# A two-layer hybrid decoder on one core: other places for the steps of prepared units, tables and scores, and more units turned by TensorE

## The chip, the core and the metric

The kernel runs on one core of a Trainium2 chip. The metric is the device time of one execution in microseconds; lower is better. TensorE is called PE, VectorE DVE, ScalarE ACT, GpSimd POOL and SyncE SP, as in the profile.

## The reference

Two layers over x of 256 positions and 2048 channels, all in float32:

```python
h = rms_norm(x, mix_norm[l]);  proj = h @ w_in[l]            # -> q, k, v, u and v of the SGU, gate logits
q, k = rope(rms_norm(q)), rope(rms_norm(k))                  # 16 query heads, 4 key heads, width 64
branch_a = sliding_window_attention(q, k, v, sinks) @ w_attn_branch[l]   # window 128
branch_b = (u * (tril(w_s) @ layer_norm(v) + b_s)) @ w_sgu_branch[l]     # u, v through gelu; chunks of 128
x = x + (gate_a * branch_a + gate_b * branch_b) @ w_out[l]   # gates: sigmoid of the logits
h2 = rms_norm(x, ffn_norm[l])
x = x + (silu(h2 @ w_gate[l]) * (h2 @ w_up[l])) @ w_down[l]  # inner width 5632
```

## The kernel before

**Products.** All products of activations and weights run as float32 split in two: a weight piece becomes whi (rounded, by ACT, line 203) and wlo (the rest, by DVE, line 204), an activation piece uh and ul, and PE adds three products, whi with uh, wlo with uh, whi with ul (lines 289 to 291). The activations stand still in PE, turned so that channels lie on partitions; weights of 512 columns are streamed. The weights come as one long list of pieces of 256 rows by 512 columns, called entries here, 1010 in all; PE takes one after the other. For an entry that serves both halves of the 256 positions PE runs 12 matmuls. `Stream.next` loads pieces 7 entries ahead by SP's queue and splits them 4 entries ahead (W_SPLIT = 4); there are four whi and four wlo tiles (pool `wsp`).

**Units.** The activations of 512 channels, split and turned, are a unit. `transposed` makes one, in either of two ways. With `on_pe` PE turns it with eight transposes into PSUM (pt, line 398), and ACT and DVE split it from there. Otherwise DVE transposes blocks of 32 by 32 into a box (`turn`, line 357), 16 DMAs of POOL's queue gather the blocks into tt (line 362), and ACT and DVE split tt. There is one box tile for all turns.

**Units with four sums.** Pairs of products (gate and up; neighbouring columns of w_out and of w_down) use a scheme that saves one of eight products over the first 512 channels. For it the first unit of such a group (WINO = 0) is made in more steps: ACT copies tt into flat in two steps (`scaled`), ACT and DVE split flat into uh and ul, DVE forms four sums of 128 by 256 (line 438), and ACT and DVE split the sums into sh and sl (`finished`, line 429 and 430). DVE also forms four sums of weight pieces for each pair (line 191). Within a pair the accumulator of one half is copied out twice by ACT, into a tile called snap (line 315), before PE adds on to it.

**Order.** PE's order is written out by hand. Small work beside the products is put in place with `after(n, fn)`: fn is called n steps later, a step being 12 matmuls, and its instructions are issued behind the latest split of that time (`tick`). ACT, DVE, POOL and SP then run the order that a scheduler made of this; each engine's queue runs in order.

**Stages of a layer.** The input projection (kv, two q, v, u and gate chunks), beside which attention and the spatial gating run in steps: rotation of q and k, turning, then from Q_FIRST = 14 steps after a q chunk the scores (psc, line 683), five steps later the transposes of the weights (ppt), three steps later the weighted values (po, line 722). Then the products of the attention branch, the second gates and the gating branch; the output projection in two pairs (`residual`), whose chunks also feed the four units of the next norm (`Norm.unit`); eleven pairs of gate and up (`hidden`) in rounds of 4, 4 and 3, each followed by two pairs of w_down over the units of that round. Only the last unit of the round of three is turned by PE, and of the norms the last unit, in the second layer's first norm the last two. `prepare` loads a layer's small rows by POOL's queue, and six steps later `tables` multiplies the rotation tables by the q and k norm weights; for the second layer that begins 20 steps after the first layer's output projection.

## Time and profile before

| | |
|---|---|
| median of 3 runs | 2565.43 us (2562.68 to 2568.48) |
| the profiled execution | 2568.65 us, its span 2566.9 us |
| mean granted PE clock in it | 0.986 |
| PE busy | 2496.1 us (97%), 11102 instructions |
| DVE busy | 1912.0 us (74%) |
| ACT busy | 1341.9 us (52%) |
| weights and inputs read | 475.27 MB, 186 GB/s over the span |

In the lists of waits a row tells who waited for whom, then the total, the times and the longest in microseconds. In a table of stretches a row has the stretch, its length, then for PE, PE's weight loads, DVE, ACT and POOL the busy time and the number of instructions, the granted clock, the DMA share and GB/s. In a list in order of time a row has start, duration, engine, line, operation, and in brackets the idle time before it with what ended it. Lines are those of the kernel before.

### The profile page before, as it was taken

The page shows a single profiled execution, that of the slowest core. Times are in us where ns is not written, and L with a number is a line of the kernel's source. Part 1 is how long each engine was busy: PE and PEld are TensorE (multiplying, and loading weights), DVE is VectorE, ACT ScalarE, POOL GpSimd, SP SyncE. Part 2 cuts the span into 40 slices and gives each one's busy share as a digit, 9 for nine tenths or more (in the row PEclk, how much of TensorE's full clock was granted, in tenths as well). Part 3 has the DMA queues.
Part 4 walks back from the last instruction along what each step waited for, and adds up shares of the span by engine and source line. Part 5 has one row for each costly group of instructions (what it writes and reads, how often), then busy time and mean ns, then how long its engine had stood idle before and what let it go on. Part 6 is the DMA issues. An engine that isn't in the chain of part 4 may idle for free. (4 is left out here: it accounts for less than half of the span.)

```text
span 2566.9 us, 31129 instructions
## 1 busy us (share of the span) xinstructions
PE 2496.1 (97%) x11102; PEld 2055.7 (80%) x11102; DVE 1912.0 (74%) x2291; ACT 1341.9 (52%) x1658; POOL 420.4 (16%) x815
## 2 busy tenths in 40 slices
PE   9899999999899999999998999999999999999999
PEld 7788888878787878787877888888787888788877
DVE  6686556887777778687976865567887777877787
ACT  5455444565555555455644554445655555555554
POOL 2401222121120112001124012221211201120110
PEclk9999999999999999999999999999999999999999
DMA  8655666565575757566666556665666666575754
GB/s 282 190 157 171 199 206 211 187 215 189 188 223 170 224 166 227 171 211 192 214 193 191 157 172 198 207 209 177 219 193 192 222 192 209 185 232 181 222 166 154
DMA packets 274123, 504.62 MB, mean 197 GB/s; under 512 B 27248, under 2 KB 29904, under 8 KB 273968
## 3 DMA queue, kind: packets, MB, share of 16 engines
q1 hardware_dynamic: 248720, 476.90, 58.8%
q0 software_dynamic: 24928, 25.47, 3.4%
q8 instruction: 87, 1.43, 0.2%
q14 instruction: 68, 0.56, 0.1%
q10 hardware_dynamic: 320, 0.27, 0.0%
HBM read 475.27 MB, written 2.10 MB: 186 GB/s over the span
## 5 line engine op out<-in xcount | busy, mean ns | idle before, releaser
L204 DVE TENSOR_TENSOR wlo<-raw,whi 128x1024 fp32r<-128x1024 f32 (+1 forms) x1012 | 1229.1, 1220 | 572.9 <-ACT whi L203 562.4
L203 ACT ACTIVATE whi<-raw 128x1024 fp32r<-128x1024 f32 (+1 forms) x1012 | 1065.8, 1058 | 1054.7 <-PE acc L291 861.8
L289 PE MATMUL acc<-whi,uh 128*128 128x512 f32 x3204 | 1261.6, 394 | 8.0 <-ACT uh L380 3.3
L291 PE MATMUL acc<-whi,ul 128*128 128x512 f32 x3204 | 1254.9, 392 | 7.4 <-DVE ul L381 4.8
L290 PE MATMUL acc<-wlo,uh 128*128 128x512 f32 x3204 | 1254.5, 392 | 1.2 <-DVE wlo L204 1.2
L291 PEld LDWEIGHTS acc<-whi,ul 128*128 128x128 f32 x3204 | 605.8, 189 | 137.4 <-DVE ul L381 6.5
L289 PEld LDWEIGHTS acc<-whi,uh 128*128 128x128 f32 x3204 | 606.9, 189 | 135.9 <-ACT uh L380 4.2
L290 PEld LDWEIGHTS acc<-wlo,uh 128*128 128x128 f32 x3204 | 606.8, 189 | 129.4 <-DVE wlo L204 4.1
L362 POOL DMA_DIRECT2D tt<-box x736 | 362.1, 499 | 1753.5 <-DVE box L357 561.3
L191 DVE TENSOR_TENSOR raw<-raw,raw 128x1024 f32<-128x1024 f32 x152 | 185.4, 1220 | 0.8
L289 PE MATMUL acc<-whi,sh 128*128 128x512 f32 x304 | 122.3, 402 | 35.1 <-ACT snap L315 35.1
L291 PE MATMUL acc<-whi,sl 128*128 128x512 f32 x304 | 121.9, 401 | 0.0
L290 PE MATMUL acc<-wlo,sh 128*128 128x512 f32 x304 | 121.4, 399 | 0.0
L315 ACT ACTIVATE snap<-acc 128x512 f32<-128x512 f32 x114 | 68.0, 596 | 59.5 <-PE acc L291 59.5
L289 PEld LDWEIGHTS acc<-whi,sh 128*128 128x128 f32 x304 | 58.4, 192 | 50.4 <-ACT snap L315 38.5
L291 PEld LDWEIGHTS acc<-whi,sl 128*128 128x128 f32 x304 | 58.8, 193 | 12.6
L290 PEld LDWEIGHTS acc<-wlo,sh 128*128 128x128 f32 x304 | 58.7, 193 | 11.8
L812 DVE SCALAR_TENSOR_TENSOR xs<-acc,xs 128x512 f32<-128x512 f32 (+1 forms) x66 | 42.5, 668 | 9.9 <-PE acc L291 9.9
L883 DVE TENSOR_TENSOR snap<-acc,snap 128x512 f32<-128x512 f32 x66 | 45.3, 686 | 4.5 <-PE acc L291 4.2
L812 DVE SCALAR_TENSOR_TENSOR xs<-snap,xs 128x512 f32<-128x512 f32 (+1 forms) x50 | 33.0, 663 | 2.1 <-ACT snap L315 2.0
L687 DVE TENSOR_TENSOR pr<-psc,mask 128x256 f32<-128x256 f32 (+1 forms) x32 | 17.3, 552 | 23.1 <-PE psc L683 23.1
L381 DVE TENSOR_TENSOR ul<-tt,uh 128x512 fp32r<-128x512 f32 x52 | 33.5, 683 | 0.0
(134 smaller groups left out, 891.2 us busy)
## 6 DMA issues: line engine op xcount, KB each, us to landing
raw<-in_w_in_dram SPq DMA_DIRECT2D x239, 512.0 KB, 4.0
raw<-in_w_up_dram SPq DMA_DIRECT2D x176, 512.0 KB, 4.9
raw<-in_w_gate_dram SPq DMA_DIRECT2D x176, 512.0 KB, 4.3
raw<-in_w_down_dram SPq DMA_DIRECT2D x176, 512.0 KB, 4.5
raw<-in_w_out_dram SPq DMA_DIRECT2D x64, 512.0 KB, 4.7
tt<-box POOLq DMA_DIRECT2D x736, 32.0 KB, 4.3
raw<-in_w_attn_branch_dram SPq DMA_DIRECT2D x32, 512.0 KB, 4.0
raw<-in_w_sgu_branch_dram SPq DMA_DIRECT2D x32, 512.0 KB, 4.4
```

The source lines that it names most:

```text
L191: self.last = nc.vector.tensor_tensor(out=self.raws[d], in0=self.raws[x], in1=self.raws[y], op=ALU.add if op == "+" else ALU.subtract)
L203: nc.scalar.activation(hi[:, i, :], raw[:, i, :], AF.Copy)
L204: self.last = nc.vector.tensor_tensor(out=lo[:, i, :], in0=raw[:, i, :], in1=hi[:, i, :].bitcast(F32), op=ALU.subtract)
L289: nc.tensor.matmul(ps, a, hi[:, kk, :], start=first and kk == 0, stop=False, skip_group_check=True)
L290: nc.tensor.matmul(ps, a, lo[:, kk, :], start=False, stop=False, skip_group_check=True)
L291: nc.tensor.matmul(ps, b, hi[:, kk, :], start=False, stop=kk == 1, skip_group_check=True)
L315: nc.scalar.activation(p.snaps[tag], a[1], AF.Copy)
L362: nc.gpsimd.dma_start(dst[j * B:(j + 1) * B, i], box[i * B:(i + 1) * B, j])
L381: nc.vector.tensor_tensor(out=l, in0=s_, in1=h.bitcast(F32), op=ALU.subtract)
L687: nc.vector.tensor_tensor(out=pr[:, :, j, :nk], in0=pscore[:, :, :nk], in1=mk.unsqueeze(1).to_broadcast([P, 2, nk]), op=ALU.add)
L812: nc.vector.scalar_tensor_tensor(out=xs[:, t, sl], in0=part[:, i * w:(i + 1) * w], scalar=scale, in1=xs[:, t, sl], op0=ALU.mult, op1=ALU.add)
L883: nc.vector.tensor_tensor(out=x[1], in0=x[0], in1=x[1], op=ALU.add)
```

## The change

Four things, with no change to what is computed:

- A unit with four sums takes its six steps (two copies, the split, two halves of the sums, the split of the sums) at distances of its own for each of the three kinds: WINO_NORM, WINO_MIX and WINO_HID. Before, they were 6, 7, 8 (split and all sums) and 9 for all.
- `tables` runs in two steps, five and six steps after `prepare`, and the second layer's `prepare` comes 28 instead of 20 steps after the output projection.
- Q_FIRST is 16 instead of 14, so scores, weighted values and the turn of the attention output come two steps later.
- The last unit of every round of hidden units is turned by PE (four more), three steps after its product, and so is unit 1 of the second layer's first norm; the last unit of that norm is turned two instead of three steps after its chunk.

```diff
+WINO_NORM = 7, 8, 10, 11, 12, 13
+WINO_MIX = 6, 7, 9, 10, 11, 13
+WINO_HID = 7, 8, 17, 18, 19, 20
...
-Q_FIRST = 14
+Q_FIRST = 16
...
-        def sums():
-            split_(uh, ul, flat["a"])
-            flat["s"] = ss = slot([P, 4, 2, P], name="sums")
+        def sums(n):
+            if n == 0:
+                flat["s"] = slot([P, 4, 2, P], name="sums")
+            ss = flat["s"]
...
-                                  (2, a11, a21, ALU.subtract), (3, a12, ss[:, 1], ALU.subtract)):
+                                  (2, a11, a21, ALU.subtract), (3, a12, ss[:, 1], ALU.subtract))[2 * n:2 * n + 2]:
...
-        after(6, lambda: scaled(0))
-        after(7, lambda: scaled(2))
-        after(8, sums)
-        after(9, finished)
+        for n, fn in zip(wino, (lambda: scaled(0), lambda: scaled(2), lambda: split_(uh, ul, flat["a"]),
+                                lambda: sums(0), lambda: sums(1), finished)):
+            after(n, fn)
...
-        after(6, pl.tables)
+        after(5, lambda: pl.tables(0))
+        after(6, lambda: pl.tables(1))
...
-                after(3 if j == NCH - 1 else 2, lambda: nxt.unit(j, j == NCH - 1 or j == NCH - 2 and not nxt.wino))
+                after(3 if j == NCH - 1 and nxt.wino else 2, lambda: nxt.unit(j, j == NCH - 1 or j > 0 and not nxt.wino))
...
-            after(2 + (j == NCH - 1), lambda j=j: transposed(mT, j, ga[j], on_pe=j == NCH - 1, wino=j == WINO))
+            after(2 + (j == NCH - 1), lambda j=j: transposed(mT, j, ga[j], on_pe=j == NCH - 1, wino=WINO_MIX if j == WINO else None))
...
-            after(20, lambda: prepare(l + 1))
+            after(28, lambda: prepare(l + 1))
...
-                pe = c == len(hT) - 1 == 2
-                after(3 if pe else 2, lambda: transposed(hT, c, hid, on_pe=pe, wino=c == WINO))
+                pe = c == len(hT) - 1
+                after(3 if pe else 2, lambda: transposed(hT, c, hid, on_pe=pe, wino=WINO_HID if c == WINO else None))
```

More of the change, by code (lines that the diff above doesn't have):

```diff
@@ L365, in turn, with transposed @@
         after(1, lambda: (blocks(1), gather()))
-    def transposed(units, c, src, cols=None, on_pe=False, wino=False):
+    def transposed(units, c, src, cols=None, on_pe=False, wino=None):
         uh = slot([P, 4, S], F32R, "uh")
@@ L466, in unit @@
             transposed(self.units, c, xs[:, :, c * CW:(c + 1) * CW], cols=self.cols[:, 4 * c:4 * c + 4],
-                       on_pe=on_pe, wino=self.wino and c == WINO)
+                       on_pe=on_pe, wino=WINO_NORM if self.wino and c == WINO else None)
         def finish(self):
@@ L557, in fetch, with tables, signs @@
                     self.lnb = dst
-        def tables(self):
+        def tables(self, i):
+            l, gn = self.l, self.gn
+            if i == 0:
+                self.signs()
+            ca = lay.tile([P, NT, 2, H2], F32, tag=f"ca{i}", name=f"ca{l}_{i}")
+            sa = lay.tile([P, NT, 2, H2], F32, tag=f"sa{i}", name=f"sa{l}_{i}")
+            for t in range(NT):
+                for hf in range(2):
+                    g_same = gn[:, i, hf * H2:(hf + 1) * H2]
+                    g_other = gn[:, i, (1 - hf) * H2:(2 - hf) * H2]
+                    nc.vector.tensor_tensor(out=ca[:, t, hf, :], in0=cs[:, t, :], in1=g_same, op=ALU.mult)
+                    nc.vector.scalar_tensor_tensor(out=sa[:, t, hf, :], in0=sn[:, t, :],
+                                                   scalar=-1.0 if hf == 0 else 1.0, in1=g_other,
+                                                   op0=ALU.mult, op1=ALU.mult)
+            self.rope.append((ca, sa))
+        def signs(self):
             l, gn = self.l, self.gn
@@ L564, in tables @@
             self.rope = []
-            for i in range(2):
-                ca = lay.tile([P, NT, 2, H2], F32, tag=f"ca{i}", name=f"ca{l}_{i}")
-                sa = lay.tile([P, NT, 2, H2], F32, tag=f"sa{i}", name=f"sa{l}_{i}")
-                for t in range(NT):
-                    for hf in range(2):
-                        g_same = gn[:, i, hf * H2:(hf + 1) * H2]
-                        g_other = gn[:, i, (1 - hf) * H2:(2 - hf) * H2]
-                        nc.vector.tensor_tensor(out=ca[:, t, hf, :], in0=cs[:, t, :], in1=g_same, op=ALU.mult)
-                        nc.vector.scalar_tensor_tensor(out=sa[:, t, hf, :], in0=sn[:, t, :],
-                                                       scalar=-1.0 if hf == 0 else 1.0, in1=g_other,
-                                                       op0=ALU.mult, op1=ALU.mult)
-                self.rope.append((ca, sa))
         def spatial(self):
```

## The prediction

> **What bounds the kernel now.** I read the page first, then the chain that ended last, the waits of PE alone, a table of stretches around each long wait, and the instructions in order of time at three of them.

> ```profile
> span 2566.9 us, 31129 instructions
> PE 2496.1 (97%) x11102; PEld 2055.7 (80%) x11102; DVE 1912.0 (74%) x2291; ACT 1341.9 (52%) x1658; POOL 420.4 (16%) x815
> ```

> PE is busy in 97% of the span, no other engine in more than 80%. So only two things can move the time: work that PE does, and gaps of PE. The waits of PE (us in total, times, longest us) name the gaps:

> ```profile
> PE acc L289 <- ACT snap L315: 35.1, 8, 7.7
> PE psc L683 <- ACT qT L667: 14.1, 2, 7.1
> PE acc L291 <- DVE ul L381: 4.8, 4, 1.4
> ```

> A gap costs more than its idle time. Stretches around every gap (us; busy us and count by engine; PEclk is the granted clock), with an undisturbed one last:

> ```profile
> 94.00:110.00 16.00, 8.89 (x34) 6.95 (x33) 8.55 (x13) 3.35 (x5) 6.22 (x8) 0.79 0.37 116
> 550.00:560.00 10.00, 6.78 (x23) 5.19 (x22) 7.58 (x14) 4.68 (x8) 4.36 (x9) 0.83 0.57 180
> 640.00:656.00 16.00, 8.32 (x29) 6.39 (x28) 11.06 (x21) 4.42 (x7) 0.00 (x0) 0.79 0.38 118
> 769.00:783.00 14.00, 10.91 (x35) 8.12 (x34) 8.09 (x9) 5.33 (x7) 0.00 (x0) 0.76 0.13 39
> 910.00:922.00 12.00, 7.26 (x26) 5.46 (x25) 8.59 (x10) 4.14 (x5) 0.00 (x0) 0.86 0.47 140
> 1035.00:1049.00 14.00, 10.91 (x35) 8.13 (x34) 8.10 (x9) 5.11 (x7) 0.00 (x0) 0.76 0.12 37
> 1176.00:1188.00 12.00, 7.27 (x26) 5.52 (x25) 8.61 (x10) 4.14 (x5) 0.00 (x0) 0.86 0.45 148
> 1298.00:1312.00 14.00, 10.67 (x40) 8.12 (x39) 8.27 (x27) 5.49 (x11) 1.09 (x2) 0.76 0.33 103
> 1378.00:1394.00 16.00, 8.96 (x35) 7.00 (x34) 8.53 (x12) 3.41 (x10) 6.84 (x9) 0.79 0.37 118
> 1743.00:1749.00 6.00, 4.23 (x19) 3.19 (x18) 4.69 (x6) 4.17 (x8) 0.00 (x0) 1.00 0.27 90
> 1836.00:1848.00 12.00, 8.77 (x32) 6.75 (x31) 9.31 (x16) 5.74 (x9) 4.42 (x9) 0.86 0.60 181
> 1926.00:1940.00 14.00, 9.92 (x33) 7.61 (x33) 9.04 (x11) 5.38 (x7) 0.00 (x0) 0.76 0.44 136
> 2052.00:2056.00 4.00, 3.02 (x13) 2.19 (x13) 4.00 (x5) 1.60 (x3) 0.00 (x0) 1.00 0.00 2
> 2187.00:2199.00 12.00, 8.30 (x29) 6.32 (x29) 8.56 (x10) 4.74 (x7) 0.00 (x0) 0.86 0.42 133
> 2312.00:2316.00 4.00, 3.02 (x14) 2.17 (x12) 4.00 (x5) 1.55 (x2) 0.00 (x0) 1.00 0.02 4
> 2447.00:2459.00 12.00, 8.29 (x30) 6.43 (x29) 8.18 (x9) 4.83 (x7) 0.00 (x0) 0.86 0.43 132
> 1100.00:1140.00 40.00, 40.00 (x178) 33.13 (x177) 29.35 (x28) 20.79 (x23) 0.00 (x0) 1.00 0.62 196
> ```

> The last row gives the pace. A matmul's record lasts 0.39 us and the next starts about 0.23 us later, so a window counts 1.7 too many: 40/(178 - 1.7) = 0.227 us each. The first number after the stretch is its length T, the first x the matmuls. What a stretch lost, idle time and slow clock together, is T - (x - 1.7) * 0.227. I call the weight pieces that PE takes in turn entries: one is 12 matmuls, 2.72 us (half that for the entries of the four sums).

> Why PE waits is seen at one place (start us, us, engine, line):

> ```profile
> 646.03 0.42 DVE L438 TENSOR_TENSOR sums<-sums,flat 128x256 f32<-128x256 f32 x1
> 647.50 0.42 DVE L438 TENSOR_TENSOR sums<-flat,sums 128x256 f32<-128x256 f32 x1
> 647.95 1.06 ACT L429 ACTIVATE sh<-sums 128x1024 fp32r<-128x1024 f32 x1 [5.00 <-DVE sums L438]
> 648.91 0.58 ACT L315 ACTIVATE snap<-acc 128x512 f32<-128x512 f32 x1
> 649.55 0.79 PE L289 MATMUL acc<-whi,sh 128*128 128x512 f32 x1 [7.68 <-ACT snap L315]
> ```

> PE waits for a copy of its accumulator (snap) that needs nothing but PE's own earlier matmul. The copy stands in ACT's queue behind sh, the split of a unit's four sums, and sh waited 5.00 us for DVE's sums. PE does not even use this sh now: it is needed a whole round later.

> A rule sorts all the gaps. The splits run four entries ahead, and there are four whi tiles, so whi of entry n+4 cannot start before PE ends entry n. Whatever stands in ACT's or DVE's queue behind that split, and is needed by PE right after entry n, stops PE. I looked in the built program for PE waits with this distance of four. In the kernel before they stand at fourteen places, and these are fourteen of the sixteen stretches above; the other two (2052, 2312) are places with distance three where a unit is split late. So I trust it to sort the changed program. There five are left: psc twice, po twice, and the gate wait at 1743.

> **The change part by part.** The sum is made against the profiled execution, 2568.65 us, which is 1.73 above its span.

> *Steps of the units with four sums at other distances.* In the changed program no snap stands behind an operation that waits for the sums: in the rounds of hidden units sh is now 14 entries behind the first snap instead of ahead of it. All eight snap places (550, 640, 910, 1176, 1836, 1926, 2187, 2447) leave the list; distance is two or less. They lost 5.2, 9.8, 6.5, 6.5, 5.1, 6.9, 5.8 and 5.6: 51.4 us gone. At 550 and 1836 it was the plain unit 1 of Norm that stood ahead of snap; it now comes some four entries earlier. The moved work itself (DVE's ul, sums and sl, ACT's uh and sh) is the same. It lies beside PE as long as DVE's lead of four entries holds; if this cover fails, a late DVE operation costs some 1.4 us (row at 774.06 below). The units are used a round later, so lateness of sh there costs nothing.

> *Layer tables in two steps, prepared 8 steps later.* The 18 small DVE operations leave the 640 stretch and land with ul of the moved unit some ten entries on.

> ```profile
> L573 DVE SCALAR_TENSOR_TENSOR sa<-sn,gn 128x32 f32<-128x32 f32 x16 | 3.0, 190 | 0.0
> ```

> I take zero, since DVE's lead of four entries (10.9 us) covers them; without it they cost at most 18 * 0.19 = 3.4 us. The three row DMAs go with them through POOL's queue, ahead of the next gather, and only the tables wait for them.

> *Last hidden units turned by PE.* Rounds of four used DVE blocks and 16 POOL DMAs for the last unit; now PE turns it. Its use was late at 769, 1035 (6.5 each), 2052 (1.4) and 2312 (1.2): 15.6 us. In the changed program the turn stands nine entries before the use, and these distances are gone. It comes three steps behind its product, as in the round of three, where PE's waits show none for it. PE pays for it:

> ```profile
> 1764.46 0.87 PE pt L398 x8
> ```

> *Unit 1 of the second layer's norm by PE, the last unit one step earlier.* The stretch at 1298 lost 14 - 0.87 - (32 - 1.7) * 0.227 = 6.3 us (8 of its 40 are transposes), waiting for unit 1's splits behind entry n+3 and n+4. Now they are eight entries ahead: 6.3 us gone. The last unit's turn moves one entry forward; its xs is ready by then, since two DVE updates behind PE's accumulator are all it needs. With the four hidden units PE gets five turns more: 5 * 0.87 = 4.4 us added. POOL loses 80 gathers, off the path.

> *Scores two steps later.* First their stretch now:

> ```profile
> 101.90 1.15 ACT L667 ACTIVATE qT<-tt 128x512 f32<-128x512 f32 x2 [5.28 <-DMA tt<-box]
> 102.58 1.62 PE L683 MATMUL psc<-kT,qT 64*128 64x128 f32 x8 [7.11 <-ACT qT L667]
> 1419.28 1.07 PE psc L683 x8
> ```

> With 8 psc at 1.07 in each, the stretches at 94 and 1378 lost 16 - 1.07 - 24.3 * 0.227 = 9.4 and 9.2 us: 18.6. Two entries later PE arrives 5.4 us later, at about the time the gather has landed (101.90). But qT stands again behind the split of distance four, so a gap stays. The nearest rows for such a gap:

> ```profile
> 769.85 0.39 PE L291 MATMUL acc<-whi,ul 128*128 128x512 f32 x1
> 770.27 1.06 ACT L203 ACTIVATE whi<-raw 128x1024 fp32r<-128x1024 f32 x1 [1.66 <-PE acc L291]
> 771.90 0.50 PE L289 MATMUL acc<-whi,uh 128*128 128x512 f32 x1 [1.67 <-ACT uh L380]
> 772.18 1.22 DVE L204 TENSOR_TENSOR wlo<-raw,whi 128x1024 fp32r<-128x1024 f32 x1
> 774.06 0.79 PE L291 MATMUL acc<-whi,ul 128*128 128x512 f32 x1 [1.42 <-DVE ul L381]
> 103.84 0.42 DVE L687 TENSOR_TENSOR pr<-psc,mask 128x256 f32<-128x256 f32 x1 [5.97 <-PE psc L683]
> ```

> One whi and one ACT operation: 1.67 idle, 1.9 against the pace. So psc keeps 1.9 each (1.7 to 2.6 if the gather lands late).

> The change also makes a new wait of distance four, in each layer: the first po (weighted values), three entries after the second psc, takes an accumulator whose reader, the second score's pr on DVE, now stands behind wlo of entry n+4. DVE's other work for that entry is queued behind it, and PE waits. Price, from the start of PE's last matmul: 0.42 until whi, 1.06, 0.1, wlo 1.22, pr 0.42, less one pace: 3.0 us each (2.8 to 3.3), 6.0 in all. Behind it DVE has its largest pile (scores, gelu of v, copies of the spatial weights), and two later psc wait for its att at distance two: 0 to 4 us a layer; I take 1.5 each, the row nearest being the 1.42 above, so 3.0.

> *The clock.* The stretch at 769 had two idle times of 1.67 and 1.42 us and got 0.76; that at 1743 had one gap of about 1.9 us (6 - 17.3 * 0.227 = 2.1 lost) and kept 1.00. The new 3.0 us gap lies between. A clock loss here costs 0.24 * 14 = 3.4 us at most; I take half of it for each of the two po, 3.4 in all, none for psc.

> [...]

> The gate place at 1743 stays as it is. Sum: gone 51.4 + 15.6 + 6.3 + 18.6 = 91.9. Back: psc 3.8, po 6.0, pile 3.0, clock 3.4, turns 4.4 = 20.6. Net 71.3: 2568.65 - 71.3 = 2497.4. The profiled execution lies 3.2 above the median of 2565.43, so 2494 on the scale of the median.

> **The rivals.** *The freed time comes back as DVE lateness* (0.12). DVE was busy for 11.06 of the 16 us at 640, most of which PE stood, and the same work now falls among splits that PE needs. Against it: the splits themselves were never late at those places, only snap. If each of the eight units and the two attention stages gave a late split of about 3 us, with half a clock loss (1.7), 47 less the 9 already counted come back: 2532; with half of that, 2513.

> *The sums were not what held snap* (0.04): snap then waits on, for whi in front of it, and the change does not do there what it says. 51.4 stays: 2545. Against it: the row at 648.91 starts when sh ends.

> *Slower* (0.04): the attention output's last unit comes late. Its turn moves two entries back while the product that reads it does not move; in the changed program its splits stand behind entry 87 and PE needs it at 90, 8 us in hand. It decides from a gather 8 us longer than now, and makes the kernel slower if PE waits over 36 us a layer for it; with 40 it gives 2574. Against it: the q gather, of the same form, landed by 101.90 in a stretch that waited 5.28 us for it.

> **How the numbers follow.** My forecast has 0.80 and gives 2494. With the lower bounds (psc 1.7, po 2.8, no pile, no clock loss) 78.5 net would give 2487; with the upper ones (psc 2.6 with a clock loss of 1.7, po 3.3 with 3.4, pile 4) 91.9 - 8.6 - 13.4 - 8 - 4.4 = 57.5 net, 2508. The three runs before lie 3 us to either side. 2481 to 2515 takes these in and half of the first rival. A measurement of this kernel tells 0.2% (5 us) from no change: all cases but the slower one are faster, 0.96, of which I leave 0.01 to no change: faster 0.95, same 0.01, slower 0.04.

> **What would show it.** In the changed profile: snap gone from PE's waits; psc on qT twice at about 1.7 to 2; po on DVE's pr twice at about 3; 40 more pt of 0.87 for 8; the gate wait unchanged; granted clock 0.995 or more instead of 0.986. I am wrong if PE's waits for wlo or ul grow by tens of us, or if snap still stands behind an ACT wait.

## The result, and the profile after

| | before | changed |
|---|---|---|
| median us | 2565.95 (2562.68 to 2568.48, 4 runs) | 2497.70 (2496.32 to 2499.61, 4 runs) |
| ratio, 95% interval | | 0.9735 (0.9718 to 0.9752) |
| the profiled execution us | 2568.65 | 2499.61 |
| mean granted PE clock in it | 0.986 | 0.995 |

The forecast was 2494 with a range of 2481 to 2515. On the scale of the profiled execution it was 71.3 us less; the profiled executions differ by 69.0.

From the page of the changed kernel (busy us, share of the span, instructions):

```profile
span 2497.9 us, 31092 instructions
PE 2479.3 (99%) x11142; PEld 2050.1 (82%) x11142; DVE 1905.9 (76%) x2281; ACT 1340.8 (54%) x1658; POOL 379.3 (15%) x735
```

PE has 40 instructions more and is busy in 99% of the span. Its waits in the changed kernel (us in total, times, longest us; the lines are some 3 to 9 further down than before):

```profile
PE po L731 <- DVE pr L696: 5.7, 2, 2.8
PE psc L692 <- ACT qT L676: 3.4, 2, 1.7
PE acc L292 <- ACT gate L808: 1.8, 1, 1.8
PE acc L292 <- ACT uh L388: 1.3, 1, 1.3
...
PE acc L293 <- DVE wlo L207: 0.8, 2, 0.5
```

The wait for snap, 35.1 us before, is gone, and so are those for ul. What the prediction said would be left is there: psc twice, po twice, gate once. The wait for uh lies in the first microseconds. The groups of instructions show why snap is free: ACT's sh used to sit idle before the sums of DVE and now does not. The first row is of before, the second of the changed kernel (busy us, mean ns, then the idle time before it and its releaser):

```profile
L429 ACT ACTIVATE sh<-sums 128x1024 fp32r<-128x1024 f32 x10 | 10.5, 1052 | 12.5 <-DVE sums L438 12.5
```

```profile
L433 ACT ACTIVATE sh<-sums 128x1024 fp32r<-128x1024 f32 x10 | 10.5, 1045 | 0.4 <-DVE sums L443 0.4
```

The same ten splits take the same time; only what they wait for differs. The stretches that still lose time, in the table of stretches of the changed kernel (columns as before: length, five engines, granted clock, DMA share, GB/s): psc and po of the first layer, the same two of the second, gate.

```profile
97.00:109.00 12.00, 10.25 (x42) 8.07 (x41) 9.07 (x13) 4.94 (x9) 3.38 (x2) 0.86 0.55 163
125.00:141.00 16.00, 13.17 (x54) 10.47 (x52) 9.36 (x16) 7.07 (x16) 0.00 (x0) 0.79 0.35 99
1337.00:1349.00 12.00, 10.34 (x42) 8.11 (x41) 9.69 (x14) 5.12 (x12) 2.26 (x1) 0.86 0.50 142
1365.00:1379.00 14.00, 11.17 (x45) 9.12 (x45) 8.20 (x16) 6.50 (x16) 0.00 (x0) 0.76 0.39 112
1697.00:1703.00 6.00, 4.23 (x19) 3.17 (x18) 5.11 (x6) 4.15 (x7) 0.00 (x0) 1.00 0.29 87
```

The clock column gives what slow clock cost: (1 - 0.86) * 12 = 1.7 us at each psc, (1 - 0.79) * 16 = 3.4 and (1 - 0.76) * 14 = 3.4 at the two po, nothing at the gate. The first po in order of time is the wait that the change made, in the steps that the prediction listed:

```profile
127.19 0.39 PE L294 MATMUL acc<-whi,ul 128*128 128x512 f32 x1
...
127.61 1.06 ACT L206 ACTIVATE whi<-raw 128x1024 fp32r<-128x1024 f32 x1 [1.66 <-PE acc L294]
...
128.70 1.22 DVE L207 TENSOR_TENSOR wlo<-raw,whi 128x1024 fp32r<-128x1024 f32 x1 [1.49 <-ACT whi L206]
129.84 0.75 DVE L696 TENSOR_TENSOR pr<-psc,mask 128x256 f32<-128x256 f32 x2
130.41 0.87 PE L731 MATMUL po<-kv,pT 128*128 128x64 f32 x3 [2.83 <-DVE pr L696]
```

PE's last matmul frees a whi tile, ACT fills it, DVE makes wlo, only then pr, and po starts: 2.83 us idle by the records. The forecast of 3.0 counts from the start of that matmul, less one pace: 130.41 - 127.19 - 0.227 = 2.99 us.

### The profile page after: what moved, and what is told of

It is laid out like the page before. It is cut to its first block, busy times and chain, and to the rows that moved or that the text cites. A ratio compares the mean times of both kernels' runs of the same rounds, so it can differ in the third digit from the quotient of the medians.

```text
span 2497.9 us, 31092 instructions
## 1 busy us (share of the span) xinstructions
PE 2479.3 (99%) x11142; PEld 2050.1 (82%) x11142; DVE 1905.9 (76%) x2281; ACT 1340.8 (54%) x1658; POOL 379.3 (15%) x735
## 4 chain that ended last, share of the span: by engine, by line
PE 97%; DMA 1%; DVE 1%; issue 0%; ACT 0%; POOL 0%; SPq 0%; DVEq 0%; ACTq 0%
PE acc L292 31%; PE acc L293 31%; PE acc L294 31%; PE po L731 1%; DMA tt<-box 1%; PE psc L692 1%; PE pt L402 1%; PE ppt L721 1%; PE psg L795 0%; POOL tt L365 0%; DVE wlo L207 0%; ACT whi L206 0%; DMA raw<-in_w_in_dram 0%; DVE ul L393 0%; PE pw L591 0%
## 5 line engine op out<-in xcount | busy, mean ns | idle before, releaser
L365 POOL DMA_DIRECT2D tt<-box x656 | 321.7, 497 | 1724.1 <-DVE box L360 650.0
L905 DVE SCALAR_TENSOR_TENSOR hid<-snap,rr,hid 128x512 f32<-128x512 f32 x44 | 32.5, 739 | 0.0
L709 ACT ACTIVATE pr<-pr,negm 128x128 f32<-128x128 f32 (+1 forms) x64 | 28.2, 442 | 7.9 <-DVE negm L702 7.9
```

Of the source, the lines that this page charges most:

```text
L365: nc.gpsimd.dma_start(dst[j * B:(j + 1) * B, i], box[i * B:(i + 1) * B, j])
L709: nc.scalar.activation(pr4[:, h, :nk], pr4[:, h, :nk], AF.Exp, bias=nm_[:, h:h + 1], accum_out=den[:, h:h + 1])
L905: nc.vector.scalar_tensor_tensor(out=hid[:, t, :], in0=up[t], scalar=norm.rr[t], in1=hid[:, t, :], op0=ALU.mult, op1=ALU.mult)
```

## The experiments

The first six kernels are the kernel before with one edit each; the other six start from the changed kernel. They ran in three groups, each beside runs of the kernel before (medians 2565.87, 2565.10 and 2566.04); gains are against the median of the group, and the interval is that of the ratio.

**The distances alone.** Only the six steps of the units with four sums move.

```diff
-        after(6, lambda: scaled(0)); after(7, lambda: scaled(2)); after(8, sums); after(9, finished)
+WINO_NORM = 7, 8, 10, 11, 12, 13;  WINO_MIX = 6, 7, 9, 10, 11, 13;  WINO_HID = 7, 8, 17, 18, 19, 20
```

> The kernel before with the steps of the units with four sums at the new distances, and nothing else changed. Theory (places): the eight places where snap stands behind sh, or behind the splits of a plain unit, cost 51.2 us together in the trace of before (5.1, 9.9, 6.6, 6.6, 5.1, 6.8, 5.6, 5.5) and nothing comes back: 51 us less than before, 2515, with no PE wait for snap left and the waits of PE for qT, uh, ul and gate as before. Rival 1 (load): the sums are late because DVE is crowded by block transposes and copies, so the distances alone move the wait and bring only part, 20 to 35 us less, and PE's waits for wlo or ul grow. Rival 2 (together): the gain of the whole change is one of its parts together, and this part alone brings under 20 us.

Measured 2509.63 (2507.72 to 2510.79), ratio 0.9779 (0.9765 to 0.9792): 56.2 us less. The waits of PE:

```profile
PE psc L691 <- ACT qT L675: 12.9, 2, 6.8
PE acc L294 <- DVE ul L385: 4.8, 4, 1.4
PE acc L292 <- ACT uh L384: 3.3, 2, 1.7
```

Snap is not among them, wlo has 1.4 us in all: no trace of the two rivals. The gain is 5 us above the sum of the eight places, at places that this edit does not touch: psc waits 1.2 us less in this execution (12.9 for 14.1), and the same idle times of the last hidden units, 1.67 and 1.42 us at 1036, had the granted clock at 1.00 where it was 0.76 before (last section).

**The last hidden units alone.**

```diff
-                pe = c == len(hT) - 1 == 2
+                pe = c == len(hT) - 1
```

> The kernel before with the last unit of every round of hidden units turned by PE, and nothing else changed. Theory (places): the places at 769, 1036, 2053 and 2313 of the trace of before cost 6.5, 6.5, 1.3 and 1.3 us and go; four turns of 0.87 us are added to PE: 12 us less, 2554. PE's wait for snap stays at 35 us in 8 times. Rival 1 (load): with 8 block transposes of DVE and 64 gathers fewer, the sums come earlier too and the wait for snap shrinks: 20 to 40 us less. Rival 2: the turns cost PE more than 0.87 each because its sequence is broken and the splits read PSUM: less than 6 us.

Measured 2552.08 (2549.35 to 2554.72), ratio 0.9946 (0.9934 to 0.9958): 13.8 us less, for 12 expected. Snap waits exactly as before, so taking this much load off DVE and POOL does nothing for it:

```profile
PE acc L292 <- ACT snap L318: 35.1, 8, 7.7
```

**The scores alone.**

```diff
-Q_FIRST = 14
+Q_FIRST = 16
```

> The kernel before with the scores two steps later, and nothing else changed. Theory (places): the two stretches at psc lost 9.6 and 9.2 us before; in the profile of the changed kernel 3.7 each are left, and the first po behind the second psc loses 6.5 and 6.4 in place of them: 18.8 gone, 20.3 back, so within 3 us of before, and most likely 1 to 2 us more (2567). My sum before the result had it as 2 us less. Rival 1 (order alone): the po wait is not caused by the later scores but by another part of the change, and then this alone is 11 us less. Rival 2: part of the two po waits is hidden elsewhere when the rest is undone: 5 us less.

Measured 2561.64 (2558.08 to 2563.05), ratio 0.9982 (0.9973 to 0.9991): 4.2 us less. My number had po waiting in both layers. It waits in one:

```profile
PE po L730 <- DVE pr L695: 2.8, 1, 2.8
```

With the second po's 6.4 us left out, 18.8 gone and 13.9 back make 4.9 less. In this kernel's built program the second layer's po indeed stands at distance three and not four; I had read the distance in another build. The two layers' stretches in the table of stretches:

```profile
124.00:140.00 16.00, 13.17 (x57) 10.40 (x56) 9.39 (x17) 7.17 (x16) 0.00 (x0) 0.79 0.30 95
1411.00:1421.00 10.00, 9.88 (x57) 7.72 (x56) 8.39 (x17) 7.07 (x16) 0.00 (x0) 1.00 0.45 138
```

The same 57 matmuls take 16 us in one layer and 10 in the other.

**The second layer's first norm alone.**

```diff
-                after(3 if j == NCH - 1 else 2, lambda: nxt.unit(j, j == NCH - 1 or j == NCH - 2 and not nxt.wino))
+                after(3 if j == NCH - 1 and nxt.wino else 2, lambda: nxt.unit(j, j == NCH - 1 or j > 0 and not nxt.wino))
```

> The kernel before with unit 1 of the second layer's first norm turned by PE and the last unit of that norm one step earlier, and nothing else changed. Theory (places): the place at 1299 lost 6.3 us, one turn of 0.87 is added: 5.4 us less, 2560.5. Rival: it is the last unit's turn that holds PE there, and a step earlier it waits for the residual of its chunk: no change, or up to 3 us slower.

Measured 2558.58 (2557.37 to 2560.76), ratio 0.9973 (0.9961 to 0.9984): 7.3 us less, for 5.4 expected, which lies in the interval. PE's wait for ul in the stretch at 1298, 2.6 us before, is not in its list any more.

**The tables alone.** `tables` in two steps at 5 and 6, `prepare` of the second layer at 28.

```diff
-        after(6, pl.tables)
+        after(5, lambda: pl.tables(0)); after(6, lambda: pl.tables(1))
-            after(20, lambda: prepare(l + 1))
+            after(28, lambda: prepare(l + 1))
```

> The kernel before with the layer tables in two steps and the second layer's small rows loaded 8 steps later, and nothing else changed. The stretch at 641 of the trace of before idles 7.85 us, that of the same kind in the second layer, where no tables are made (1927), 4.24. Theory (queue): in the kernel before, DVE's 18 table operations lie ahead of the sums that hold sh and snap, so moving them alone takes 3.6 us of that idle time away, and up to 1.7 more of slow clock: 4 us less, 2562, and the 641 wait is then 4.2. Rival (no effect): the sums there wait for something else, the wait stays 7.8, and the time is that of before. In the whole change, where snap no longer waits for the sums, this part is worth nothing by either.

Measured 2561.65 (2557.39 to 2565.54), ratio 0.9988 (0.9979 to 0.9998): 3.4 us less, and the longest wait for snap went from 7.7 to 4.7:

```profile
PE acc L292 <- ACT snap L318: 32.1, 8, 4.7
```

So the table operations stood ahead of the sums. In the whole change this is not a gain of its own, since the distances take all of that wait away.

**One number: only the last step later.** From the kernel before, sums in one piece.

```diff
-        after(9, finished)
+        after(13, finished)
```

> The kernel before with one number changed: the last of the six steps of a unit with four sums (sh and sl made from the sums) comes at step 13 instead of 9, for all three kinds; the copies, the split and the sums stay in one piece at steps 6, 7 and 8. Theory (queue): what stopped PE was only that sh, which waits for the sums, stood ahead of snap in ACT's queue. DVE is as crowded as before and the sums are as late, but snap's eight waits go and the time is that of the kernel with all the distances changed, 2510 (2507 to 2515). Rival (crowding): the sums in one piece ahead of the weight splits make wlo late, so a good part of the 56 us comes back as waits for wlo, 2525 or more.

Measured 2512.15 (2510.44 to 2513.59), ratio 0.9796 (0.9781 to 0.981): 53 us less. In the edit only sh and sl move, and sh no longer waits:

```profile
L433 ACT ACTIVATE sh<-sums 128x1024 fp32r<-128x1024 f32 x10 | 10.4, 1045 | 0.0
```

At six of the eight places ACT's queue differs as the edit says: sh, which stood right ahead of snap, now stands behind it. At the other two (550 and 1836) sh was not what held snap. There the plain unit's split uh stood between the refill and snap, as the prediction says, and the scheduler's order for this kernel has that uh four weight splits earlier, though the edit does not name it. The first two rows are of before, the last two of this kernel:

```profile
552.54 1.69 ACT L384 ACTIVATE uh<-tt,vcols 128x256 fp32r<-128x256 f32 x4
554.13 0.57 ACT L315 ACTIVATE snap<-acc 128x512 f32<-128x512 f32 x1
```

```profile
541.00 1.69 ACT L388 ACTIVATE uh<-tt,vcols 128x256 fp32r<-128x256 f32 x4
545.08 0.58 ACT L318 ACTIVATE snap<-acc 128x512 f32<-128x512 f32 x1
```

So this run shows that the order of ACT's queue is what costs, and for six places that it is the place of sh. For the other two, 12.1 of the forecast 51.4 us, it shows the place of uh, and why the scheduler moved that is not shown. The kernel is 2.5 us slower than with all the new distances by the medians, 3.3 by the gains of the two groups. One wait of 0.7 us for wlo, right behind DVE's table operations at the first hidden unit, is seen in its trace; the rest is within the spread of the runs. So the other moves of the distances, the separate sums among them, are worth some 2.5 to 3.3 us.

**The changed kernel with the old distances.**

```diff
-WINO_NORM = 7, 8, 10, 11, 12, 13;  WINO_MIX = 6, 7, 9, 10, 11, 13;  WINO_HID = 7, 8, 17, 18, 19, 20
+WINO_NORM = WINO_MIX = WINO_HID = 6, 7, 8, 8, 8, 9
```

> The changed kernel with the old distances of the units with four sums (6, 7, 8 for split and all sums, 9), the rest of the change kept. Theory (places add up): snap's eight waits come back, the one of the first layer that had 7.9 us at 4.3 to 4.9, since the tables are no longer ahead of its sums: 51.2 less 3 to 5 is 47 us more than the changed kernel, 2545. Rival (parts lean on each other): with the last hidden units off DVE's and POOL's queues the sums are early enough, and less than half of it comes back: under 2522.

Measured 2537.76 (2535.76 to 2539.91), ratio to before 0.989 (0.9876 to 0.9905): 40.1 us more than the changed kernel. Against 47 expected, 6.4 are missing, and again it is one po:

```profile
PE acc L292 <- ACT snap L318: 32.1, 8, 4.7
...
PE po L731 <- DVE pr L696: 2.8, 1, 2.8
```

The second layer's po is at distance four only in builds that have the norm's edit and not in all of those: its place in DVE's order is the scheduler's, and hangs on edits far away.

**The changed kernel with the scores at 14.**

```diff
-Q_FIRST = 16
+Q_FIRST = 14
```

> The changed kernel with the scores back at 14 steps, the rest kept. In its built program psc's wait on qT stands at distance four, po's on pr at three. Theory: psc loses 8 to 9.5 us a layer for 3.7, po nothing for 6.5, so 16 to 19 lost for 20.3: 1 to 4 us less than the changed kernel, 2494 to 2497; the later scores bring nothing in the whole change. Rival (my prediction's sum): the later scores are worth 18.6 - 3.8 - 6 - 3 - 3.4 = 2.4 us, so 2500.

Measured 2497.91 (2497.25 to 2498.54), ratio to before 0.9735 (0.972 to 0.9749): the same as the changed kernel, a little above what I expected and below the rival. psc waits longer, po not at all:

```profile
PE psc L692 <- ACT qT L676: 13.1, 2, 6.6
```

So within the whole change the later scores are worth nothing: they take away the long waits of psc with their slow clock and pay with 7.4 us at psc and 12.9 at po.

**The changed kernel without the norm's edit.**

```diff
-                after(3 if j == NCH - 1 and nxt.wino else 2, lambda: nxt.unit(j, j == NCH - 1 or j > 0 and not nxt.wino))
+                after(3 if j == NCH - 1 else 2, lambda: nxt.unit(j, j == NCH - 1 or j == NCH - 2 and not nxt.wino))
```

> The changed kernel with the second layer's first norm as before (its unit 1 by block transposes, its last unit a step later), the rest kept. In its built program the second layer's po wait stands at distance three and the norm's own wait at four again. Theory: 5.4 to 6.3 us come back at the norm and 6.4 go at the second layer's po: 2497, the same as the changed kernel within 2 us. Rival: po waits as before by 2.8 us, and the kernel is 6 us slower, 2504.

Measured 2495.89 (2495.38 to 2496.11), ratio to before 0.9727 (0.9712 to 0.9741): 1.8 us less than the changed kernel. The norm waits again and one po has gone:

```profile
PE po L731 <- DVE pr L696: 2.8, 1, 2.8
PE acc L294 <- DVE ul L393: 2.3, 1, 2.3
```

An edit that brings 7.3 us alone brings nothing here, because it tips the other layer's po over.

**Five tiles.**

```diff
-    big = ctx.enter_context(tc.tile_pool(name="big", bufs=25))
+    big = ctx.enter_context(tc.tile_pool(name="big", bufs=23))
-    wsp = ctx.enter_context(tc.tile_pool(name="wsp", bufs=4))
+    wsp = ctx.enter_context(tc.tile_pool(name="wsp", bufs=5))
```

> The changed kernel with five whi and five wlo tiles instead of four, the splits still four entries ahead; to make room for them the pool of large tiles has 23 instead of 25. In its built program psc's two waits on qT now stand at distance five, po's two on pr and the gate's one at four as before. Theory (the distance counts tiles): a wait stops PE where its distance is the number of tiles, so psc's two waits of 1.7 us stay, po's two of 2.8 and the gate's of 1.8 go, with their clock loss: 15 us less than the changed kernel, 2483. Rival (the place itself is late, whatever the tiles): po and gate wait on, 2497. Third (room): the smaller pool makes new waits, 2500 or more.

Measured 2484.28 (2481.68 to 2485.41), ratio to before 0.9683 (0.9667 to 0.9699): 13.4 us less than the changed kernel, where 15 were expected. The waits of PE:

```profile
PE psc L692 <- ACT qT L676: 3.4, 2, 1.7
PE acc L292 <- ACT uh L388: 1.9, 2, 1.2
PE acc L293 <- DVE wlo L207: 1.8, 4, 0.6
```

The order of the wait at po and at gate is the same as in the changed kernel, and both waits are gone; psc, whose distance went to five with the tiles, waits its 1.7 us as before. The mean granted clock of this execution was 1.000, with psc's two gaps of 1.7 us still in it. This is the sharpest of the tests: it is the number of tiles, not the place, that turns a distance into a stop. The pool of large tiles is smaller here too, and no run has that alone; the waits that went and stayed are those that the distance names.

**The queries turned one step earlier.**

```diff
-Q_TURN = 7
+Q_TURN = 6
```

> The changed kernel with the turn of the queries one step earlier (Q_TURN 6 for 7), and nothing else changed. In its built program the wait of po on pr stands at distance three in both layers, the wait of psc on qT still at four. Theory (distance): the two po waits of 2.8 us go with their clock loss, 12.9 us in all, the two psc waits of about 1.7 stay: 2485. Rival (DVE pile): the second score's pr is late because DVE is crowded there, so po waits on for 2 us or more at each place: 2492 to 2498.

Measured 2485.90 (2484.26 to 2488.74), ratio to before 0.9695 (0.968 to 0.9709): 11.8 us less than the changed kernel, po gone, psc left:

```profile
PE psc L692 <- ACT qT L676: 3.6, 2, 1.9
```

**Both turns earlier, scores later still.**

```diff
-K_TURN = 7; Q_TURN = 7; Q_FIRST = 16
+K_TURN = 6; Q_TURN = 6; Q_FIRST = 19
```

> The changed kernel with the keys' and the queries' turn one step earlier (K_TURN and Q_TURN 6 for 7) and the scores three steps later (Q_FIRST 19 for 16). In its built program no wait of PE in the attention stage stands at distance four. Theory (distance): psc's and po's four waits go with their clock loss, 7.4 and 12.9 us: 2477. Rival (late last unit, the one that my prediction had for slower): the turn of the attention output comes 3 steps (8 us) later; if its gather is not in by then, PE waits for uh or ul of that unit in both layers and 10 to 20 us come back: 2487 to 2497.

Measured 2479.70 (2479.42 to 2481.02), ratio to before 0.9671 (0.9656 to 0.9685): 18 us faster than the changed kernel, and the fastest here. No wait of the attention stage is left, and the clock stays full (PE's waits, then the core's span and mean granted clock):

```profile
PE acc L293 <- DVE wlo L207: 2.0, 5, 0.6
PE acc L292 <- ACT gate L808: 1.8, 1, 1.8
PE pwarm L253 <- DVE warm L248: 1.1, 1, 1.1
PE acc L292 <- ACT uh L388: 0.4, 1, 0.4
```

```profile
core 0: 2478.0 us, clock 1.000
```

It is also the test of the rival that the prediction had for slower. The turn of the attention output is three steps later than in the changed kernel, and its last unit is still not waited for. Which of the three numbers frees psc is not separated here.

## Why the prediction was right

**What held.** The sorting rule held at every place. Of fourteen waits with distance four, those that the changed program no longer has are gone, the five that it has are there, and nothing else came. The rival of DVE lateness fell: PE waits 0.8 us for wlo in the changed kernel and not at all for ul. The four parts that carry the gain brought, each alone, 56, 14, 4 and 7 us where I had 51, 12, 2 and 5. For the scores the agreement is luck: alone they lack one of the two po waits, and in the whole change they bring nothing where I had 2.

**Snap.** The second rival, that the sums were not what held snap, fell too: at six places the sums held sh, and sh held snap; at 550 and 1836 it was the plain unit's uh, as I had read. That it was the queue and not a crowded DVE is shown by the one number (53 us), which leaves DVE the same work and changes ACT's order ahead of snap at all eight places. The slower rival would have needed a late last attention unit; no such wait is in the list, nor three steps later still.

**Terms of the sum, forecast and measured**, all in what comes back, 20.6 in the sum:
- The clock. I gave psc none and each po half of 3.4. Both psc got 1.7, both po the whole 3.4: 10.2 for 3.4. This is one execution and the slowest of four: its granted clock of 0.995 stands against 0.997 in the other three, so in those the term was smaller.
- The pile on DVE behind po: 0 for 3.0. No psc waits for att in the list above.
- psc and po themselves came as forecast: 3.4 and 5.7 of idle by the records are 3.7 and 6.0 against the pace, for 3.8 and 6.0.
- The turns: 40 more, at 0.87 for eight, as forecast; one of the added ones in the chain of the changed kernel:

```profile
734.06 0.87 PE pt L402 x8
```

So 7.4 for psc with its clock, 12.9 for po with its own, and 4.4 for the turns come to 24.7. That is 4.1 more than the forecast, while the profiled executions lie only 2.3 off the sum; the 1.8 between came from places outside the sum. Of it 1.0 lies at the start, where the 301st matmul of the products begins at 83.40 us for 84.44 before; the rest I have not followed. On the scale of the medians the forecast is 3.7 off. That it is so close is partly luck: the clock cost 6.8 more than I had, the pile 3.0 less, and the 1.8 has no place in my sum. The tables were costed at nothing in the whole change, though alone they bring 3.4. That fits the run of the distances alone, where snap does not wait with the tables in their old place; no run takes the tables alone out of the changed kernel.

**Idle gaps and the clock.** In the changed kernel 2.83 us of idle at each po were followed by slow clock (0.79 over 16 us and 0.76 over 14), and so were 1.75 and 1.67 us at the two psc (0.86 over 12 us each); the gate's 1.77 us were not (1.00 over 6).

**What the parts add up to.** The five parts alone sum to 84.9 us, the whole is 68.3 (its own two medians). Of the 16.6 between, 3.0 is the tables' wait, which the distances take away as well, and 6.4 the second layer's po, which waits in the whole but in none of the five. The other 7 are spread over the start and the clock, a few us for each kernel, and I have not settled them.

## What to carry to other kernels

Where a producer refills a ring of tiles for the bottleneck engine, count for each of that engine's other waits how many refills stand ahead of the awaited operation in its queue: at the number of tiles PE stopped here (fourteen places with four tiles; with five, po's 2.8 us and the gate's 1.8 were gone), below it did not unless the operation itself was late (two places at distance three in the kernel before idled 0.97 us each), and the built program tells this without a run. What need not be early goes behind what must be, even by one step; an operation that itself waits, as sh did for 5.00 us ahead of snap, is the worst to put ahead. Count again after every edit, since an unrelated one can move a wait over the edge.

## What the runs showed of the hardware

```profile
1008.00:1022.00 14.00, 10.91 (x47) 8.39 (x47) 10.76 (x11) 6.19 (x8) 0.00 (x0) 1.00 0.17 42
```

PE's busy time is the same 10.91, the clock is full, and 12 more matmuls got done. In the kernel with the tables alone a wait of 3.2 us for snap left no mark, where the same wait in the kernel before had 0.86 over 12 us:

```profile
1830.00:1840.00 10.00, 6.78 (x30) 5.29 (x29) 8.71 (x16) 5.41 (x10) 3.98 (x9) 1.00 0.57 179
```

I cut PE's idle time in the traces of before and after, from 60 us to 5 us before PE's end, into steps of 3.413 us that begin where the stretches at half clock do. Of the steps at full clock, all fourteen with 2.26 us idle or more were followed by one at half clock, and none with 1.36 or less was. Between these, 1.67, 1.75 and 1.78 us were followed by half clock and 1.69, 1.84, 1.86 and 1.94 were not, and what decides there is not shown. In the changed kernel the wait of 2.83 us at po fell as 2.67 and 0.16 us into two steps in the first layer and as 2.26 and 0.57 in the second; each time 6.83 us at half clock began with the second step. The gate's 1.77 us fell as 1.02 and 0.76, in the kernel before as 1.36 and 0.42, and kept the full clock in both.

So a gap of 1.7 or 1.8 us cost nothing more or 1.7: the gate's kept the full clock, psc's lost it in both layers of the changed kernel (0.86 over 12 us) and in neither with five tiles (mean granted clock 1.000). One of 2.8 to 3.2 us cost nothing (snap with the tables alone), 1.7 (the same wait before) or 3.4 (po in the changed kernel). A forecast for this kernel should carry that span for each gap, and a difference of a few us between two of these kernels may be only this.
